# A second pair of feed-forward tiles by eight products, its token sums spread over it, and modulation tied to given VectorE operations

## The chip, the cores and the metric

The kernel runs on one core of a Trainium2 chip. The metric is the device time of one execution in microseconds (us), as the median of several runs; the profile and trace come from one further execution of the same program. Engine names are those of the profile: PE is TensorE, PEld its weight loads, DVE is VectorE, ACT is ScalarE, POOL is GpSimd, SP is SyncE, which issues the DMAs.

## The reference, cut to what matters

A trunk of two layers works on 512 latent and 256 context tokens, 1024 channels wide. Each layer is a feed-forward network (FFN), a token mixer and a second FFN. All have an RMS norm with a shift, scale and gate that come from a linear map of the conditioning vector (the "modulation"). The change touches the FFNs and the modulation alone:

```
def modulate(h, g, shift, scale):
    return rms_norm(h, g) * (1 + scale[:, None]) + shift[:, None]

def swiglu(h, w_in, w_out):
    a, b = jnp.split(h @ w_in, 2, axis=-1)
    return (jax.nn.silu(a) * b) @ w_out

mod_x = sc @ w_mod[l] + b_mod[l]                      # 9 groups of 1024 per layer
x = x + 0.5 * mx[2][:, None] * swiglu(modulate(x, norm_g, mx[0], mx[1]), ffn_in, ffn_out)
```

The inner width is 2816, which is 22 tiles of 128 rows. Four FFNs are computed; the last one (second FFN of the last layer) works on the 512 latent tokens alone, the other three on all 768.

## The kernel before, in words

**Number format.** Each operand is split into a high and a low part (`split`, L72: ACT copies the high part, DVE subtracts to get the low part), and each product is three matmuls (high by high, high by low, low by high). A weight of 128x512 that goes through `operand` (L167) so costs one ACT copy (`whi`) and one DVE subtraction (`wlo`). There are five rooms for such pairs, four for raw weights (L163), and six PSUM banks for products (L146).

**An FFN** (`ffn`, L449) goes over the 22 inner tiles in six parts of 2, 4, 4, 4, 4 and 4 (`PARTS`). For each part the input products make the gated tiles `g`, and then `out_product` (L296) multiplies them by eight output weights `j` and adds each result, times the gate `hg`, to the residual `X` (`resid`, L288, on DVE, which also frees the PSUM bank).

**Eight or seven products.** Part 0 goes by `ffn_tiles` (L320): plain products, in two stretches of tokens (512 and 256). Every later pair of tiles goes by `ffn_seven` (L381): the pair is a 2x2 block product (two tiles by two halves of the channels by two halves of the tokens), made of seven block products in place of eight. For that it needs sums of weights (POOL, rooms `ws`, L418 to L436) and sums of tokens. The token sums (`token_sums`, L345, once for each `k` of 0 to 3) are DVE operations on 128x384 (L356 and L359) with splits on ACT and DVE into the rooms `T`; one of them overwrites half of `h` itself in place (`hi[k][:, b]`, `lo[k][:, b]`). In program order the sums of `k` = 0, 1, 2 stand between `ffn_tiles` and the output products of part 0, those of `k` = 3 after its second output weight. The seven products stand in the order 1, 6, 5, 2, 7, 3, and product 4 is put off until after product 1 of the next one (`self.defer`).

**Modulation.** `mod_tile` (L193) loads 512 KB of `w_mod` through SP into one of two rooms `wm` and does two DVE operations (L200, `junk<-wm,cb`, 128x1024, with a sum of the row). The first FFN has 56 such tiles, of which the first eight (`early`) make its own gate `hg`, 40 go with the second FFN and 32 with the third, the last has none. They are told one after another by `background`, whose shares spread them over parts 1 to 5.

**The order of the work** on every engine is fixed when the program is built: the scheduler of the framework simulates the engines and puts on each, when it is free there, the first ready instruction in program order. What is ready early may so be placed far ahead of where it was told. On the chip each engine then runs its queue in that order.

The four FFNs are called A (layer 0, first), B (layer 0, second), C (layer 1, first) and D (layer 1, second) below; OUT0 is the output product of part 0, P1 to P5 are the parts 1 to 5, each with its input products and its output products. A mixer follows A and C; the weights of its first products are loaded and split on POOL (`start_mix`, L540) into space that `self.mod_room.close()` (L498) and the end of the rooms `T` give back.

Of the kernel before, what the change touches and what calls it, by code (L numbers as in the profile page):

```python
# [12 lines left out]
ALU = mybir.AluOpType  # L13
# [39 lines left out]
class Net:  # L53
# [182 lines left out]
    def norm_squares(self, sg):  # L236
# [3 lines left out]
        if self.hold:  # L240

            acc = self.mp.tile([128, 512], F32, tag="cb", name="acc", bufs=1)
        else:
            acc = self.wp.tile([128, 512], F32, tag="ws", name="acc", bufs=3)
# [73 lines left out]
    SPARE = ((("gp", "gh2", 1), ("gp", "gl2", 1)), (("gp", "gh3", 1), ("gp", "gl3", 1)), (("wp", "ws", 3), ("wp", "ws", 3)))  # L318

    def ffn_tiles(self, l, f, i0, g, h, segs):  # L320
# [13 lines left out]
        for sg in segs:  # L334
            for i in range(2):
                a, b = [self.product(ws[i, ab], h, sg, KD) for ab in range(2)]
                sa = self.ep.tile([128, 512], F32, tag="e", name="sa")[:, :sg.stop - sg.start]
                nc.scalar.activation(out=sa, in_=a, func=AF.Silu)
                nc.vector.tensor_tensor(sa, sa, b, op=ALU.mult)
                self.split(g[0][i][:, sg], g[1][i][:, sg], sa)  # L340
# [4 lines left out]
    def token_sums(self, h, nt, k):  # L345
# [8 lines left out]
        def whole(i, sl):  # L354
            z = self.ep.tile([128, NT // 2], F32, tag="c", name="t", bufs=8)[:, :m]
# [3 lines left out]
        sub = lambda o, x, y: nc.vector.tensor_tensor(o, x, y, op=ALU.subtract)  # L359
        t1, t3 = whole(k, a), whole(k, b)  # L360
# [3 lines left out]
        sub(t3, t2, t3)  # L364
        self.split(hi[k][:, b], lo[k][:, b], t3)
# [15 lines left out]
    def ffn_seven(self, l, f, i0, g, gi, B, nt, background):  # L381
# [4 lines left out]
        c = lambda n: self.ep.tile([128, NT // 2], F32, tag="c", name=n, bufs=8)[:, :m]  # L386
# [20 lines left out]
        for ab in range(2):  # L407
            r0, r1 = [self.raw(self.A["ffn_in"][l, f, i0 + i, ab], KD) for i in range(2)]
            a11, a12, a21, a22 = r0[:, 0:4], r0[:, 4:8], r1[:, 0:4], r1[:, 4:8]
            S = lambda: self.wp.tile([128, 4, 128], F32, tag="ws", name="ws", bufs=3)  # L410
# [11 lines left out]
            nc.vector.tensor_tensor(u2, s1, p6, op=ALU.add)  # L422
            mult(p5, self.operand(w1), 5, True, True)
# [3 lines left out]
            done(ab, "11", p1)  # L427
            w3 = S()
            nc.gpsimd.tensor_tensor(w3, a11, a21, op=ALU.subtract)
            mult(p6, self.operand(w3), 7, False, True)  # L430
# [4 lines left out]
            w4 = S()  # L435
            nc.gpsimd.tensor_tensor(w4, a12, w2, op=ALU.subtract)  # L436
            mult(p5, self.operand(w4), 3, False, True)
            nc.vector.tensor_tensor(u2, u2, p5, op=ALU.add)
            done(ab, "12", u2)
# [7 lines left out]
            background(1.0)  # L447
# [1454 lines left out]
```

## Time and profile before

| | us |
|---|---|
| median of 3 runs | 3454.74 (3453.64 to 3459.22) |
| profiled execution, its own time | 3451.14 |
| its span, first to last instruction | 3449.0 |

| engine | busy us | share of the span |
|---|---|---|
| PE | 3171.4 | 92% |
| DVE | 2502.3 | 73% |
| ACT | 1318.1 | 38% |
| POOL | 984.7 | 29% |

The profile counts an engine as busy while one of its instructions runs. A busy PE is not PE at its peak: its matmuls overlap, and their spacing tells the pace. The mean granted clock of TensorE is 0.936 of its full speed. The stages are told apart by the names of the tiles in the trace: input products read `hh`, `hl` or `T`, output products read `g`.

### The profile page before, as it was taken

The page shows a single profiled execution, that of the slowest core. Times are in us where ns is not written, and L with a number is a line of the kernel's source. Part 1 is how long each engine was busy: PE and PEld are TensorE (multiplying, and loading weights), DVE is VectorE, ACT ScalarE, POOL GpSimd, SP SyncE. Part 2 cuts the span into 40 slices and gives each one's busy share as a digit, 9 for nine tenths or more (in the row PEclk, how much of TensorE's full clock was granted, in tenths as well). Part 3 has the DMA queues.
Part 4 walks back from the last instruction along what each step waited for, and adds up shares of the span by engine and source line. Part 5 has one row for each costly group of instructions (what it writes and reads, how often), then busy time and mean ns, then how long its engine had stood idle before and what let it go on. Part 6 is the DMA issues. An engine that isn't in the chain of part 4 may idle for free.

```text
span 3449.0 us, 55188 instructions
## 1 busy us (share of the span) xinstructions
PE 3171.4 (92%) x20996; PEld 2810.6 (81%) x20996; DVE 2502.3 (73%) x4755; ACT 1318.1 (38%) x2399; POOL 984.7 (29%) x816
## 2 busy tenths in 40 slices
PE   7699999899989988899999799999899879989999
PEld 6688899778778766789998688999777667778998
DVE  8999856567955348998557899555747864468777
ACT  4332334442233334323335333333434233264444
POOL 0333334144332100433221133333245432103433
PEclk9899999899889888999999899999999878889999
DMA  6354322223232022343222243222313322033333
GB/s 244 119 168 153 114 68 77 95 77 99 71 112 64 5 90 94 123 158 126 71 74 80 97 148 123 70 68 66 121 55 107 88 79 55 5 109 100 99 98 123
DMA packets 184345, 335.77 MB, mean 97 GB/s; under 512 B 64752, under 2 KB 80976, under 8 KB 183696
## 3 DMA queue, kind: packets, MB, share of 16 engines
q1 hardware_dynamic: 184080, 332.25, 30.6%
q8 instruction: 165, 2.70, 0.3%
q14 instruction: 100, 0.82, 0.1%
HBM read 304.99 MB, written 27.18 MB: 96 GB/s over the span
## 4 chain that ended last, share of the span: by engine, by line
PE 61%; DVE 24%; issue 8%; DMA 4%; ACT 2%; POOL 1%; SPq 0%; DVEq 0%; ACTq 0%; POOLq 0%
PE pt L63 39%; PE pj L63 6%; PE pr L63 6%; DVE junk L200 5%; DVE wlo L78 4%; PE sc L63 3%; PE ps L63 1%; DVE T L1282 1%; DVE inv L1284 1%; PE po L63 1%; PE pc L63 1%; PE pg L63 1%; DVE gate L398 1%; DVE g L78 1%; DVE X L290 1%
## 5 line engine op out<-in xcount | busy, mean ns | idle before, releaser
L63 PE MATMUL pt<-g,whi 128*128 128x512 f32 (+1 forms) x2528 | 642.4, 345 | 49.1 <-DVE X L290 32.1
L77 ACT ACTIVATE whi<-wraw 128x512 fp32r<-128x512 f32 (+1 forms) x616 | 371.6, 615 | 571.2 <-PE pt L63 355.4
L63 PE MATMUL pt<-hh,whi 128*128 128x384 f32 (+2 forms) x1536 | 499.5, 336 | 58.9 <-DVE u L422 28.8
L63 PEld LDWEIGHTS pt<-g,whi 128*128 128x128 f32 x2528 | 441.3, 191 | 114.0 <-DVE X L290 33.8
L63 PE MATMUL pt<-hh,wlo 128*128 128x384 f32 (+2 forms) x1536 | 502.8, 331 | 14.3 <-DVE wlo L78 14.3
L63 PE MATMUL pt<-hl,whi 128*128 128x384 f32 (+2 forms) x1536 | 506.7, 332 | 2.5 <-DVE hl L78 2.5
L78 DVE TENSOR_TENSOR wlo<-wraw,whi 128x512 fp32r<-128x512 f32 (+1 forms) x528 | 424.4, 811 | 67.7 <-ACT whi L77 63.7
L63 PE MATMUL pt<-T,whi 128*128 128x384 f32 (+1 forms) x1920 | 455.1, 324 | 3.2 <-ACT whi L77 2.1
L63 PE MATMUL pt<-g,wlo 128*128 128x512 f32 (+1 forms) x1264 | 425.8, 342 | 0.0
L200 DVE SCALAR_TENSOR_TENSOR junk<-wm,cb 128x1024 bf16<-128x1024 f32 x272 | 363.5, 1336 | 11.3 <-ACT cb L191 10.4
L63 PEld LDWEIGHTS pt<-hh,whi 128*128 128x128 f32 x1536 | 299.2, 197 | 75.6 <-DVE u L422 34.4
L418 POOL TENSOR_TENSOR ws<-wraw 128x512 f32<-128x512 f32 x80 | 125.2, 1565 | 796.5 <-DMA wraw<-in_ffn_in 405.3
L63 PEld LDWEIGHTS pt<-T,whi 128*128 128x128 f32 x1920 | 334.9, 189 | 6.4 <-ACT whi L77 3.5
L290 DVE SCALAR_TENSOR_TENSOR X<-pt,hg,X 128x512 f32<-128x512 f32 (+1 forms) x376 | 226.9, 616 | 144.8 <-PE pt L63 144.0
L77 ACT ACTIVATE whi<-ws 128x512 fp32r<-128x512 f32 x320 | 200.0, 628 | 341.7 <-PE pt L63 257.4
L63 PEld LDWEIGHTS pt<-hh,wlo 128*128 128x128 f32 x1536 | 299.5, 196 | 21.5 <-DVE wlo L78 17.1
L63 PE MATMUL pt<-T,wlo 128*128 128x384 f32 (+1 forms) x960 | 307.9, 324 | 0.8 <-DVE wlo L78 0.7
L63 PEld LDWEIGHTS pt<-hl,whi 128*128 128x128 f32 x1536 | 301.3, 196 | 8.9 <-DVE hl L78 3.9
L78 DVE TENSOR_TENSOR wlo<-ws,whi 128x512 fp32r<-128x512 f32 x320 | 258.6, 811 | 52.2 <-ACT whi L77 48.5
L63 PEld LDWEIGHTS pt<-g,wlo 128*128 128x128 f32 x1264 | 241.3, 191 | 26.8
L433 POOL TENSOR_TENSOR s<-s,u 128x384 f32<-128x384 f32 (+1 forms) x80 | 107.3, 1341 | 471.3 <-DVE u L432 412.6
L78 POOL TENSOR_TENSOR wlo<-wraw,whi 128x512 fp32r<-128x512 f32 x88 | 126.1, 1435 | 300.6 <-ACT whi L77 262.9
(444 smaller groups left out, 5759.0 us busy)
## 6 DMA issues: line engine op xcount, KB each, us to landing
wraw<-in_ffn_in SPq DMA_DIRECT2D x176, 512.0 KB, 3.4
wm<-in_w_mod SPq DMA_DIRECT2D x144, 512.0 KB, 3.4
wraw<-in_ffn_out SPq DMA_DIRECT2D x192, 256.0 KB, 2.7
wraw<-in_w_in SPq DMA_DIRECT2D x88, 256.0 KB, 2.8
wraw<-in_w_out SPq DMA_DIRECT2D x32, 256.0 KB, 3.1
xd<-X SPq DMA_DIRECT2D x16, 384.0 KB, 2.5
wraw<-in_ffn_out SPq DMA_DIRECT2D x32, 128.0 KB, 2.2
wa<-in_w_out SPq DMA_DIRECT2D x16, 256.0 KB, 3.2
```

The lines of the kernel that those rows point to most:

```text
L63: self.nc.tensor.matmul(out, lhsT=lhsT, rhs=rhs, start=start, stop=stop, skip_group_check=skip)
L77: self.nc.scalar.activation(out=hi, in_=src, func=AF.Copy)
L78: (eng or self.nc.vector).tensor_tensor(lo, src, hi.bitcast(F32), op=ALU.subtract)
L200: nc.vector.scalar_tensor_tensor(out=junk, in0=w, scalar=1.0, in1=self.cb[:, s], op0=ALU.mult, op1=ALU.mult, accum_out=self.mod[l][:, s, j ...
L290: self.nc.vector.scalar_tensor_tensor(out=self.X[j][:, sg], in0=o, scalar=self.hg[l][:, s, 8 * n + j:8 * n + j + 1], in1=self.X[j][:, sg], ...
L398: nc.vector.tensor_tensor(gate[at], gate[at], src, op=ALU.mult)
L418: nc.gpsimd.tensor_tensor(w1, a21, a22, op=ALU.add)
L433: nc.gpsimd.tensor_tensor(s5, s5, u3, op=ALU.add)
L1282: nc.vector.tensor_tensor(tv, N[:, s, tt].unsqueeze(2).to_broadcast([96, nt, nj]), X[:, s, jj].unsqueeze(1).to_broadcast([96, nt, nj]), op ...
L1284: nc.vector.tensor_tensor(X[:, tt, jj], X[:, tt, jj], tv, op=ALU.add)
```

## The change

It does five things. (1) The first pair of part 1 (tiles 2 and 3) goes by a new `ffn_plain`, eight products without sums, in the two stretches of tokens. (2) The three token sums that go into `T` are told after the output weights j = 1, 3, 5, 7 of part 0, one `k` each; the one that overwrites `h` in place is told after `ffn_plain`, and takes two further additions for each `k`, since its inputs are made again. (3) `background` ties the DVE operations of what it tells behind the DVE instruction told last; it is called four times with a quarter share in each seven in place of once with a full share. (4) In a seven, product 3 comes ahead of product 7, and its weight sum ahead of that of 7. (5) Weight sums get four rooms in place of three, and DVE's small tiles `c` six in place of eight.

```diff
@@ token_sums(self, h, nt, k, ns)
+        if 3 in ns:
+            t2, t3 = whole(4 + k, b), whole(k, b)
+            sub(t3, t2, t3)
+            self.split(hi[k][:, b], lo[k][:, b], t3)
+            return
         t1, t3 = whole(k, a), whole(k, b)
         sub(t1, t3, t1)
         self.split(T[1][0][:, k, :m], T[1][1][:, k, :m], t1)
         t2 = whole(4 + k, b)
-        sub(t3, t2, t3)
-        self.split(hi[k][:, b], lo[k][:, b], t3)
         sub(t2, t2, t1)
...
@@ new
+    def ffn_plain(self, l, f, i0, g, gi, h, segs):
+        nc = self.nc
+        for i in range(2):
+            ws = []
+            for ab in range(2):
+                raw = self.raw(self.A["ffn_in"][l, f, i0 + i, ab], KD)
+                ws.append([self.operand(raw[:, 4 * q:4 * q + 4]) for q in range(2)])
+            for sg in segs:
+                self.gated(ws, h, sg, [g[q][gi + i][:, sg] for q in range(2)])
...
@@ ffn_seven
-            S = lambda: self.wp.tile([128, 4, 128], F32, tag="ws", name="ws", bufs=3)
+            S = lambda: self.wp.tile([128, 4, 128], F32, tag="ws", name="ws", bufs=4)
...
             nc.vector.tensor_tensor(u2, s1, p6, op=ALU.add)
+            background(0.25)
             mult(p5, self.operand(w1), 5, True, True)
...
             done(ab, "11", p1)
+            background(0.25)
+            w4 = S()
+            nc.gpsimd.tensor_tensor(w4, a12, w2, op=ALU.subtract)
             w3 = S()
             nc.gpsimd.tensor_tensor(w3, a11, a21, op=ALU.subtract)
+            mult(p5, self.operand(w4), 3, False, True)
+            nc.vector.tensor_tensor(u2, u2, p5, op=ALU.add)
+            done(ab, "12", u2)
+            background(0.25)
             mult(p6, self.operand(w3), 7, False, True)
...
-            background(1.0)
+            background(0.25)
@@ ffn
-        shares = [0.0, 2.0 * (len(PARTS) * 2 - 2) + 4.0 * (len(PARTS) - 2)]
+        shares = [0.0, 2.0 * (len(PARTS) * 2 - 3) + 4.0 * (len(PARTS) - 2)]
         def background(share):
             shares[0] += share
-            while side and todo - len(side) < todo * shares[0] / shares[1]:
-                side.pop(0)()
+            if side and todo - len(side) < todo * shares[0] / shares[1]:
+                told = self.nc.cur_bb.bb.instructions
+                last = next(x for x in reversed(told) if x.engine == mybir.EngineType.DVE)
+                with self.tc.issue_after(last):
+                    while side and todo - len(side) < todo * shares[0] / shares[1]:
+                        side.pop(0)()
...
-                for k in range(3):
-                    self.token_sums(h, nt, k)
-                sums = lambda j: self.token_sums(h, nt, 3) if j == 1 else None
+                sums = lambda j: self.token_sums(h, nt, j // 2, (1, 2, 4)) if j % 2 == 1 else None
             else:
                 for i in range(0, np_, 2):
-                    self.ffn_seven(l, f, m0 + i, g, i, B, nt, background)
+                    if m0 + i == 2:
+                        self.ffn_plain(l, f, m0, g, 0, h, segs)
+                        for k in range(4):
+                            self.token_sums(h, nt, k, (3,))
+                        B = self.token_blocks(h, nt)
+                    else:
+                        self.ffn_seven(l, f, m0 + i, g, i, B, nt, background)
```

Shared code of `ffn_tiles` and `ffn_plain` moves into `gated`: one product each for the two halves of the gate, SiLU on ACT, a DVE multiplication and a split.

## Rows read from the trace of the kernel before

**Rows 1.** The profile page, chain that ended last: shares of the span by line.
```profile
PE pt L63 39%; PE pj L63 6%; PE pr L63 6%; DVE junk L200 5%; DVE wlo L78 4%; PE sc L63 3%; PE ps L63 1%; DVE T L1282 1%; DVE inv L1284 1%; PE po L63 1%; PE pc L63 1%; PE pg L63 1%; DVE gate L398 1%; DVE g L78 1%; DVE X L290 1%
```

**Rows 2.** Stretches of A: OUT0, P1, P2, P3, P4.
```profile
core 0: us, PE busy (x) PEld busy (x) DVE busy (x) ACT busy (x) POOL busy (x), PEclk, DMA share, GB/s
79.40:126.60 47.20, 20.59 (x99) 16.73 (x98) 47.20 (x92) 12.09 (x26) 8.17 (x4) 0.75 0.35 114
126.60:226.20 99.60, 95.07 (x531) 89.25 (x530) 98.39 (x156) 31.92 (x60) 35.39 (x22) 0.98 0.49 153
226.20:328.60 102.40, 95.24 (x531) 88.92 (x530) 101.05 (x160) 31.90 (x60) 34.70 (x21) 0.98 0.47 153
328.60:430.10 101.50, 94.57 (x530) 89.21 (x529) 86.97 (x134) 31.79 (x60) 33.39 (x21) 0.98 0.38 124
430.10:522.00 91.90, 91.90 (x530) 87.92 (x529) 53.27 (x84) 32.85 (x60) 27.56 (x20) 1.00 0.22 69
```

**Rows 3.** The same view of B: OUT0, P1, P2.
```profile
1361.60:1390.00 28.40, 21.38 (x97) 16.56 (x96) 28.40 (x58) 8.73 (x21) 5.97 (x3) 0.88 0.39 132
1390.00:1500.90 110.90, 99.87 (x528) 92.41 (x529) 110.45 (x172) 35.29 (x66) 38.75 (x23) 0.94 0.41 134
1500.90:1602.20 101.30, 94.76 (x530) 89.17 (x529) 100.90 (x159) 32.03 (x60) 35.74 (x21) 0.98 0.49 154
```

**Rows 4.** The same view of C: OUT0, P1, P2.
```profile
1934.00:1964.50 30.50, 21.19 (x97) 16.22 (x95) 30.50 (x59) 9.92 (x23) 4.32 (x3) 0.90 0.36 117
1964.50:2076.00 111.50, 101.09 (x529) 93.66 (x530) 110.37 (x172) 33.92 (x64) 37.62 (x22) 0.92 0.42 136
2076.00:2175.70 99.70, 94.74 (x531) 89.09 (x530) 82.79 (x126) 32.27 (x60) 31.95 (x20) 0.98 0.37 118
```

**Rows 5.** The same view of D: OUT0, P1, P2.
```profile
3106.10:3120.70 14.60, 13.13 (x51) 10.46 (x52) 14.60 (x38) 5.53 (x14) 0.00 (x0) 0.88 0.31 100
3120.70:3189.90 69.20, 64.32 (x431) 59.52 (x430) 55.03 (x81) 30.51 (x63) 31.63 (x24) 0.98 0.32 102
3189.90:3253.30 63.40, 62.02 (x433) 58.03 (x432) 48.77 (x77) 29.25 (x60) 26.78 (x20) 1.00 0.32 100
```

**Rows 6.** Input products of P3 and P4, output products of P4 (FFN A).
```profile
328.60:392.50 63.90, 56.97 (x315) 55.58 (x314) 63.90 (x95) 23.80 (x46) 25.65 (x15) 0.97 0.39 123
430.10:484.40 54.30, 54.30 (x315) 54.30 (x314) 32.72 (x50) 25.14 (x47) 19.28 (x14) 1.00 0.18 55
484.40:522.00 37.60, 37.60 (x217) 33.62 (x216) 20.55 (x34) 7.71 (x13) 8.28 (x6) 1.00 0.29 91
```

**Rows 7.** P3 of A, modulation (tile junk) alone: us, DVE busy (records), clock, DMA.
```profile
328.60:430.10 101.50, 30.40 (x44) 0.98 0.38 124
```

**Rows 8.** DVE in order of time, OUT0 of A: start, us, instruction.
```profile
101.73 3.15 DVE L359 TENSOR_TENSOR t<-t 128x384 f32<-128x384 f32 x2
...
111.54 0.16 DVE L216 TENSOR_SCALAR hg<-mod 128x16 f32<-128x16 f32 x1
...
112.76 2.18 DVE L290 SCALAR_TENSOR_TENSOR X<-pt,hg,X 128x512 f32<-128x512 f32 x4
```

**Rows 9.** Groups of DVE instructions, 1340 to 1390 us (B, end of norm and OUT0).
```profile
L200 DVE SCALAR_TENSOR_TENSOR junk<-wm,cb 128x1024 bf16<-128x1024 f32 x12 | 15.1, 1262 | 5.7 <-ACT cb L191 5.7
L359 DVE TENSOR_TENSOR t<-t 128x384 f32<-128x384 f32 x12 | 7.4, 620 | 0.0
```

**Rows 10.** The profile page, the modulation's DVE group over the whole span.
```profile
L200 DVE SCALAR_TENSOR_TENSOR junk<-wm,cb 128x1024 bf16<-128x1024 f32 x272 | 363.5, 1336 | 11.3 <-ACT cb L191 10.4
```

**Rows 11.** Waits of SP's queue, 126 to 400 us: total us, times, longest.
```profile
SPq L60 <- DVE junk L200: 133.3, 45, 6.5
```

**Rows 12.** SP, POOL and PE in order of time: first weights of A's mixer, first product.
```profile
391.42 0.80 SPq L60 DMA_DIRECT2D gS<-in_w_in  x2
...
595.15 1.65 POOL L78 TENSOR_TENSOR wh<-wa,wh 128x512 fp32r<-128x512 f32 x1
...
619.96 0.71 PE L63 MATMUL pj<-hh,wh 128*128 128x512 f32 x2 [2.94 <-ACT hh L77]
```

More of the change, by code (lines that the diff above doesn't have):

```diff
@@ L243, in norm_squares @@
         else:
-            acc = self.wp.tile([128, 512], F32, tag="ws", name="acc", bufs=3)
+            acc = self.wp.tile([128, 512], F32, tag="ws", name="acc", bufs=4)
         nc.scalar.activation(out=acc[:, :n], in_=self.X[0][:, sg], func=AF.Square)
@@ L315, in out_and_norm, with gated @@
         return h
-    SPARE = ((("gp", "gh2", 1), ("gp", "gl2", 1)), (("gp", "gh3", 1), ("gp", "gl3", 1)), (("wp", "ws", 3), ("wp", "ws", 3)))
+    SPARE = ((("gp", "gh2", 1), ("gp", "gl2", 1)), (("gp", "gh3", 1), ("gp", "gl3", 1)), (("wp", "ws", 4), ("wp", "ws", 4)))
+    def ffn_plain(self, l, f, i0, g, gi, h, segs):
[7 more added lines that the diff above has]
+                self.gated(ws, h, sg, [g[q][gi + i][:, sg] for q in range(2)])
+    def gated(self, ws, h, sg, out):
+        nc = self.nc
+        a, b = [self.product(w, h, sg, KD) for w in ws]
+        sa = self.ep.tile([128, 512], F32, tag="e", name="sa")[:, :sg.stop - sg.start]
+        nc.scalar.activation(out=sa, in_=a, func=AF.Silu)
+        nc.vector.tensor_tensor(sa, sa, b, op=ALU.mult)
+        self.split(*out, sa)
     def ffn_tiles(self, l, f, i0, g, h, segs):
@@ L335, in ffn_tiles, with token_sums @@
             for i in range(2):
[L336 to L340, printed above, removed]
+                self.gated([ws[i, ab] for ab in range(2)], h, sg, [g[q][i][:, sg] for q in range(2)])
     def token_rooms(self):
         self.T = {n: [self.tp.tile([128, 4, NT // 2], F32R, tag=f"T{n}{q}", name="T") for q in range(2)] for n in (1, 2, 4)}
-    def token_sums(self, h, nt, k):
+    def token_sums(self, h, nt, k, ns):
         nc = self.nc
@@ L354, in whole @@
         def whole(i, sl):
-            z = self.ep.tile([128, NT // 2], F32, tag="c", name="t", bufs=8)[:, :m]
+            z = self.ep.tile([128, NT // 2], F32, tag="c", name="t", bufs=6)[:, :m]
             nc.vector.tensor_tensor(z, hi[i][:, sl].bitcast(F32), lo[i][:, sl].bitcast(F32), op=ALU.add)
@@ L385, in ffn_seven @@
         a, b = slice(0, m), slice(m, nt)
-        c = lambda n: self.ep.tile([128, NT // 2], F32, tag="c", name=n, bufs=8)[:, :m]
+        c = lambda n: self.ep.tile([128, NT // 2], F32, tag="c", name=n, bufs=6)[:, :m]
         bank = lambda: self.pj.tile([128, 512], F32, tag="pj", name="pt")[:, :m]
@@ L434, in ffn_seven @@
             done(ab, "22", s5)
[L435 to L439, printed above, removed]
             def last(ab=ab, p6=p6, s1=s1, op=self.operand(a22)):
@@ L490, in ffn @@
                 self.out_product(l, n, src, g, np_, segs if nt == NT else [slice(0, nt)], between=sums)
-            if part == 0:
-                B = self.token_blocks(h, nt)
             m0 += np_
```

## The prediction

> **What bounds the kernel now.** I read the chain of waits first. PE's products lead it, but modulation on DVE (line 200) holds 5% of the span and the low parts of weights (line 78) another 4% [rows 1]. So there are places where PE waits for DVE, and the next view must say where. The table of stretches does. A part that nothing disturbs is P4 of A: 91.9 us, PE busy throughout, clock 1.00, DVE busy for 53.3 [rows 2]. P1, P2 and P3 of A hold the same matmuls (about 530) and take 99.6, 102.4 and 101.5, with DVE busy for 98.4, 101.1 and 87.0 [rows 2]. P3 shows why: its 22 modulation operations take 30.4 us [rows 7] and all lie in its input products, which have 32.7 us of other DVE work (that of P4's). 32.7 + 30.4 = 63.1, and the stretch takes 63.9 with DVE busy for all of it, against 54.3 in P4 [rows 6]. The stretch is as long as its DVE work. P4 has no modulation at all: it is bunched in the first parts because the schedule places it as soon as it is ready.
>
> The worst place is OUT0. Its bare time: P4's output stretch of 37.6 us holds 192 output matmuls and 24 of 384 columns; 384 columns cost 54.3 / 312 = 0.174 (315 records, three cut by the edges), so the 192 cost 37.6 - 4.2 = 33.4 [rows 6], and OUT0, with half as many, 16.7. In D, with the 512-column two thirds alone, it is 11.1.
>
> Excess over bare, all DVE-bound (DVE busy 100% of OUT0 in all four) [rows 2 to 5]:
> OUT0: A 47.2 - 16.7 = 30.5; B 11.7; C 13.8; D 3.5; together 59.5.
> P1 to P3: A 7.7 + 10.5 + 9.6 = 27.8; B 19.0 + 9.4 = 28.4; C 19.6 + 7.8 = 27.4 (bare 91.9 each); D 69.2 - 63.4 = 5.8; together 89.4.
> In all 148.9 us that PE loses to DVE. The mixers are not touched.
>
> **What the change adds: PE work.** The plain pair is 4 weight tiles by 8 blocks by 3 matmuls, 96 of 512 and 96 of 256 columns. These are the shapes and the number of a whole output stretch: 33.4 us. The seven that it replaces is 2 x 7 x 12 = 168 of 384 columns: 29.2. That is +4.2 in A, B and C, and two thirds of it, 2.8, in D: **+15.4 us**, on the path in full, since PE sets it there.
>
> **Token sums.** Before, twelve DVE operations for each k, at about 0.62 us [rows 9], must end before the first seven: 48 in all, some 30 us per FFN in front of and inside OUT0. Now ten for each k stay there; two (the sum that overwrites h, and its low part) go behind the plain pair, with two additions made anew. So about 5 us leave OUT0 and 4 x 4 x 0.62 = 10 us come back behind the plain pair, where product 7, five products later (10 us), is the first to read them. The plain pair itself gives 33 us of PE time with little DVE work: 8 low parts of weights and 8 gate operations, against 14 and more in a seven. That hides what is left of the sums. Were the cover gone, the 10 us would fall on PE; I take 0. POOL loses one pair's weight sums, and these no longer run beside the token sums. In OUT0 of A two token operations took 3.15 us together [rows 8], where POOL had 8.2 us of work [rows 2], against 0.62 each [rows 9].
>
> OUT0 of A is special: residual additions need the gate hg, which is ready at 111.5, and the first four follow at 112.8 [rows 8]. DVE is full until then with the eight early modulation tiles and the sums. Only the 5 us of sums, some collisions and the later modulation between the residual additions go: I take 10.5 of 30.5 (bounds 5 and 20). B: 12 modulation operations, 15.1 us [rows 9], and 5 us of sums leave the end of the norm and OUT0; I take 8 of OUT0's 11.7 and 3 in the norm before it, 11. C by analogy: 9 and 3, 12. D has no modulation and gains by the sums and the plain pair alone: 3.5 + 5.8 to 3.0, a gain of 6.3. **Together 39.8.**
>
> **Modulation tied and spread.** One operation costs 30.4 / 22 = 1.38 us with its accumulator read [rows 7]. The shares give 8/34 of the tiles to each of P2, P3, P4, half of it to the input products. For A (48 tiles) that is 11.3 tiles, 31.2 us of DVE: inputs 32.7 + 15.6 = 48.3 of 54.3 us, outputs 20.6 + 15.6 = 36.2 of 37.6. B (40 tiles): 45.7 and 33.6. C (32): 43.1 and 31.0. By these sums DVE fits under PE everywhere, in A's output stretches by little, where six PSUM banks let PE run ahead. An in-order queue will not be perfect; I leave 2 us in each of four parts of A, 7 in B and 6 in C: 27.8 + 28.4 + 27.4 - 21 = **62.6 gained** (bounds: all 83.6, and half of it).
> The waits that this adds: a modulation operation must follow the DVE instruction told before it; behind it queue the next low part of a weight and the next u, s or residual addition, and behind those PE. Its load moves with it on SP: room wm is free only after the tile two before, and raw weights queue behind that wait. SP already waits so, 45 times, at most 6.5 us [rows 11]; the raw weights have four rooms, two seven-steps' worth, so nothing.
>
> A rule speaks against the spreading. Two-input DVE operations and POOL: the row shows modulation at 1.34 us on average [rows 10] and 1.26 in a stretch with little POOL work [rows 9]. The Trainium skill, page "SBUF — State Buffer", section "Who interferes with whom", says that a DVE instruction with two SBUF inputs and a GpSimd instruction that reads SBUF exclude each other, the second blocked until the first ends. By that, 11 operations moved beside POOL's sums in P4 or P5 cost a whole POOL operation each at worst; by the rows the mean cost is 0.1 each and lies in my 1.38 already.
>
> **Small ones.** Product 3 ahead of 7 leaves product 4 only one product (2.1 us) after the DVE read of 7's bank, where it had two: cost 0 to 0.3 a seven, taken as 0, as P4 shows DVE idle for 40%. A fourth room of weight sums: POOL is at 19.3 of 54.3 [rows 6], no bound: 0. Six small DVE tiles for eight: a seven holds six at most: 0 (at worst 1 us a seven). The first weights of A's mixer were loaded at 391 [rows 12], when modulation had ended; now its room frees only with P5's inputs, near the end of A's inputs. POOL ended at 597 and PE needed it at 620 [rows 12], 23 us of cover for some 5 to 10: 0, else 10 each in A and C.
>
> **The sum.** 39.8 + 62.6 - 15.4 = 87.0. The profiled execution took 3451.1, so 3364.1. It stands 3.6 below the median of the runs, so **3368** for the median.
>
> **Rivals.**
> (a) *The queue keeps OUT0 as it is.* Token sums are ready as soon as the norm is, and the schedule already places them before they are told; it may go on putting them ahead of the residual additions. Then OUT0 gives nothing and P1 to P3 half: 89.4 / 2 - 15.4 = 29, **3425**. For it: DVE ran sums before the first residual addition in A [rows 8]. Against it: residual additions and the first sums change places in program order, and modulation leaves the stretch.
> (b) *All of it goes:* 148.9 + 6 for the norms - 15.4 = 139.5, **3315**. Against it: A's gate is late whatever is done with the sums.
> (c) *Slower.* Tied operations stand right in front of urgent ones. The place is the input products of P2 to P5; the price is x for each of the 240 tied operations (2 x 120 tiles), on PE, in place of the 83.6 lost now. Break-even: 240 x = 83.6 + 39.8 - 15.4 = 108, x = 0.45 us, a third of an operation. P3 of A pays 9.6 / 22 = 0.44 each today, so that is not far off if spreading brought nothing. At x = 0.7: 168 - 83.6 - 39.8 + 15.4 = +60, **3515**. Against it: at 48.3 of 54.3 there is slack for each, which P3 had not.
> (d) *The tie does nothing* (the operations are still bunched): the parts keep their loss but for the sums in P1, some 20 back, with 39.8: 44 net, 3410. I count it with (a).
>
> **How the numbers follow.** Forecast 0.60, own range 3340 to 3405 (A's OUT0 from 5 to 20, the spreading's residue from 10 to 40). (a) with (d) 0.18, (b) 0.12, (c) 0.10. The range of 8 in 10 reaches from half of (b) to past (a): **3325 to 3435**. A measurement of this kernel tells about 0.2% (7 us) from no change. Faster: 0.60 + 0.18 + 0.12 less a little of (a), 0.88; the same 0.03; slower 0.09.
>
> **What would show it.** Right: OUT0 of B and C near 20 us with residual additions from its first microseconds; P2 to P4 of A, B and C alike, 92 to 95 us, with DVE at 75 to 90%; modulation to the end of P5; P1 about 98. OUT0 of A still near 36, until hg. Wrong: parts of 97 us and more through P4 and P5 with PE waiting for low parts or for u and s behind modulation, which is (c); OUT0 unchanged with sums in front, which is (a); or a late first product of the mixer.

## Result: 97.2% of the time before, and where it came from

The changed kernel takes **3358.6 us** (median; 3354.4 to 3362.7), the kernel before, timed beside it, 3456.0. The ratio is **0.9717, interval 0.970 to 0.9735**. The forecast was 3368 in a range of 3325 to 3435. The profiled execution took 3361.9, span 3360.0, against 3449.0.

The chain of waits (the profile's walk back from the last instruction, at each step to what held it up) comes first again, from the profile page of the changed kernel:

```profile
PE 71%; DVE 16%; DMA 5%; ACT 3%; issue 3%; POOL 1%; SPq 1%; DVEq 0%; POOLq 0%; ACTq 0%
PE pt L63 49%; PE pj L63 7%; PE pr L63 6%; PE sc L63 3%; DVE wlo L78 2%; PE ps L63 2%; DVE junk L200 2%; PE po L63 1%; DVE T L1310 1%; DMA wraw<-in_ffn_in 1%; DVE inv L1312 1%; PE pc L63 1%; DVE X L290 1%; PE pg L63 1%; ACT t L278 1%
```

PE has 71% of the chain in engines. Modulation has gone from 5% to 2% of it and the low parts of weights from 4% to 2% [rows 1]. The stretches of A after, in the columns of [rows 2]: OUT0, P1, P2, P3, P4.

```profile
79.80:123.50 43.70, 23.26 (x98) 18.86 (x97) 41.54 (x85) 10.00 (x22) 0.00 (x0) 0.73 0.34 111
123.50:219.50 96.00, 96.00 (x554) 88.19 (x553) 67.08 (x105) 29.20 (x54) 23.94 (x16) 1.00 0.32 99
219.50:315.40 95.90, 93.71 (x530) 89.41 (x530) 87.44 (x136) 32.70 (x60) 34.59 (x20) 0.98 0.41 132
315.40:409.50 94.10, 92.18 (x531) 87.91 (x530) 83.89 (x132) 32.96 (x60) 32.98 (x20) 1.00 0.40 130
409.50:502.90 93.40, 92.14 (x530) 87.84 (x529) 85.67 (x133) 32.89 (x60) 30.66 (x20) 1.00 0.41 131
```

P2 to P4 are alike now, 93 to 96 us with DVE busy for 84 to 87, where they took 102.4, 101.5 and 91.9 with 101.1, 87.0 and 53.3. P1 is PE from end to end. OUT0 has hardly moved. The same view of B (OUT0, P1, P2) and of D (P2 alone), for [rows 3] and [rows 5]:

```profile
1344.00:1365.40 21.40, 18.01 (x99) 14.80 (x97) 21.40 (x47) 8.16 (x19) 0.00 (x0) 1.00 0.34 106
1365.40:1461.50 96.10, 96.10 (x553) 88.30 (x554) 76.05 (x122) 29.25 (x55) 26.13 (x16) 1.00 0.32 104
1461.50:1554.60 93.10, 91.96 (x530) 87.62 (x529) 78.16 (x123) 32.87 (x60) 30.05 (x20) 1.00 0.39 125
...
3088.90:3154.00 65.10, 62.46 (x434) 58.18 (x433) 49.93 (x77) 29.44 (x61) 27.01 (x21) 1.00 0.31 98
```

B's OUT0 fell to 21.4 and its P1 from 110.9 to 96.1. D's P2 did not fall: 65.1, where it took 63.4.

The table divides the profiled executions. An FFN runs here from the first matmul of its OUT0 to the last of P5. "Mixer A" and "mixer C" are what lies between A and B and between C and D, with the norms and the input products of the next part 0; the 53.2 and 49.2 us between B and C are a norm and such input products.

| us | before | after | difference |
|---|---|---|---|
| A: OUT0, P1 to P3, P4 and P5 | 47.0, 303.5, 184.5 | 43.5, 286.0, 186.0 | -19.5 |
| B, the same | 29.9, 305.1, 184.3 | 20.8, 281.5, 185.7 | -31.3 |
| C, the same | 32.7, 303.3, 184.3 | 21.5, 280.1, 186.8 | -31.9 |
| D: OUT0, P1, P2 to P5 | 14.4, 69.3, 255.5 | 13.0, 65.4, 267.6 | +6.8 |
| norm between B and C | 53.2 | 49.2 | -4.0 |
| mixer A, mixer C | 744.4, 654.4 | 748.6, 640.7 | +4.2, -13.7 |

The FFNs give 75.9 us, less than the forecast's 87 for FFNs and norms. The mixers, which the change does not touch, give 9.5 of the rest and the norm 4.0. So the forecast was close for reasons that are partly not its own, and three questions were put to the chip: which part of the change brings the gain, what D lost, and why the mixers moved.

### The profile page after: what moved, and what is told of

Its sections match the earlier page's. It is cut to its first block, busy times and chain, and to the rows that moved or that the text cites. A ratio compares the mean times of both kernels' runs of the same rounds, so it can differ in the third digit from the quotient of the medians.

```text
span 3360.0 us, 55161 instructions
## 1 busy us (share of the span) xinstructions
PE 3140.3 (93%) x21092; PEld 2787.7 (83%) x21092; DVE 2465.8 (73%) x4731; ACT 1304.0 (39%) x2359; POOL 932.3 (28%) x776
## 4 chain that ended last, share of the span: by engine, by line
PE 71%; DVE 16%; DMA 5%; ACT 3%; issue 3%; POOL 1%; SPq 1%; DVEq 0%; POOLq 0%; ACTq 0%
PE pt L63 49%; PE pj L63 7%; PE pr L63 6%; PE sc L63 3%; DVE wlo L78 2%; PE ps L63 2%; DVE junk L200 2%; PE po L63 1%; DVE T L1310 1%; DMA wraw<-in_ffn_in 1%; DVE inv L1312 1%; PE pc L63 1%; DVE X L290 1%; PE pg L63 1%; ACT t L278 1%
## 5 line engine op out<-in xcount | busy, mean ns | idle before, releaser
L63 PE MATMUL pt<-hh,whi 128*128 128x384 f32 (+2 forms) x1664 | 531.9, 329 | 36.3 <-ACT g L77 19.0
L63 PE MATMUL pt<-hl,whi 128*128 128x384 f32 (+2 forms) x1664 | 541.9, 327 | 0.7 <-DVE hl L78 0.6
L63 PE MATMUL pt<-hh,wlo 128*128 128x384 f32 (+2 forms) x1664 | 536.9, 326 | 0.5 <-DVE wlo L78 0.3
L63 PE MATMUL pt<-T,whi 128*128 128x384 f32 (+1 forms) x1728 | 406.0, 322 | 0.0
L436 POOL TENSOR_TENSOR ws<-wraw 128x512 f32<-128x512 f32 x72 | 113.3, 1574 | 1036.4 <-DMA wraw<-in_ffn_in 915.1
L63 PEld LDWEIGHTS pt<-hh,whi 128*128 128x128 f32 x1664 | 318.7, 193 | 51.7 <-ACT g L77 21.1
L63 PEld LDWEIGHTS pt<-hl,whi 128*128 128x128 f32 x1664 | 321.0, 193 | 10.8 <-DVE hl L78 1.8
L63 PEld LDWEIGHTS pt<-hh,wlo 128*128 128x128 f32 x1664 | 319.1, 193 | 9.4 <-DVE wlo L78 1.3
L63 PEld LDWEIGHTS pt<-T,whi 128*128 128x128 f32 x1728 | 300.0, 188 | 1.0
L63 PE MATMUL pt<-T,wlo 128*128 128x384 f32 (+1 forms) x864 | 276.4, 322 | 0.0
L63 PE MATMUL pj<-hh,whi 128*128 128x512 f32 x616 | 191.2, 376 | 15.0 <-DVE k L1126 8.3
```

The lines of the kernel that those rows point to most:

```text
L63: self.nc.tensor.matmul(out, lhsT=lhsT, rhs=rhs, start=start, stop=stop, skip_group_check=skip)
L436: nc.gpsimd.tensor_tensor(w1, a21, a22, op=ALU.add)
```

## Experiments

Times are medians of the timed runs, ratios stand to the kernel before. Stage figures are from one profiled execution each, divided as above; how far a stage that no edit touches can differ between two traces is told under "Why the mixers move".

**Which part gives the gain: the tie.** The tie of modulation behind a DVE instruction is taken out of the changed kernel, all else stays:

```diff
-                told = self.nc.cur_bb.bb.instructions
-                last = next(x for x in reversed(told) if x.engine == mybir.EngineType.DVE)
-                with self.tc.issue_after(last):
-                    while side and todo - len(side) < todo * shares[0] / shares[1]:
-                        side.pop(0)()
+                while side and todo - len(side) < todo * shares[0] / shares[1]:
+                    side.pop(0)()
```

> The changed kernel without the tie: modulation is told at the same places, but the schedule may place it as early as it is ready. Theory: it is bunched again in the first parts; P2 and P3 of A and P2 of B and C go back to 99 to 102 us (some 36 more together), and OUT0 and P1 of B and C lose 5 to 10 each to modulation in front: 3400 to 3420. Rival (the plain pair alone makes the gain, the tie does nothing): 3359 within 8.

Measured: 3434.6, ratio 0.9927 (0.990 to 0.995). More is lost than expected. The stretches P1 to P4 of A without the tie:

```profile
125.20:227.60 102.40, 97.69 (x554) 87.99 (x553) 98.78 (x158) 27.86 (x54) 27.39 (x16) 1.00 0.51 161
227.60:330.20 102.60, 95.46 (x530) 89.30 (x529) 102.35 (x163) 31.57 (x60) 35.42 (x21) 0.98 0.48 154
330.20:430.60 100.40, 94.55 (x531) 89.35 (x530) 77.58 (x119) 32.41 (x60) 33.36 (x20) 0.98 0.33 108
430.60:522.50 91.90, 91.90 (x531) 87.93 (x530) 53.94 (x84) 33.23 (x60) 27.32 (x20) 1.00 0.21 69
```

This is the picture of [rows 2]: DVE nearly full in P1 and P2, and P4 with no modulation at all. Quarter shares alone do not spread it. The other way round, the tie with the quarter shares put into the kernel before, without the plain pair, the spread sums, the new order and the new rooms:

```diff
-            while side and todo - len(side) < todo * shares[0] / shares[1]:
-                side.pop(0)()
+            if side and todo - len(side) < todo * shares[0] / shares[1]:
+                told = self.nc.cur_bb.bb.instructions
+                last = next(x for x in reversed(told) if x.engine == mybir.EngineType.DVE)
+                with self.tc.issue_after(last):
+                    while side and todo - len(side) < todo * shares[0] / shares[1]:
+                        side.pop(0)()
...
-            background(1.0)
+            background(0.25)
```

> The kernel before with the tie and the quarter shares alone: no plain pair, sums, order and rooms as before. Theory: P2 and P3 of A and P2 of B and C come to 93 to 95 us (33 less together), OUT0 and P1 of B and C give back the 12 to 20 modulation operations that stood there, some 15 to 20 each, A's P1 5; D stays: 3456 - 70 = 3385, range 3370 to 3405. Rival (modulation costs the same wherever it stands): 3456 within 10.

Measured: 3350.2, ratio 0.9692 (0.966 to 0.972), better than expected and no worse than the whole change. OUT0, P1 and P2 of A:

```profile
80.20:124.60 44.40, 19.95 (x97) 16.26 (x97) 42.79 (x82) 12.01 (x26) 7.07 (x5) 0.77 0.30 98
124.60:216.70 92.10, 92.10 (x531) 87.86 (x530) 84.25 (x128) 32.59 (x60) 33.63 (x21) 1.00 0.40 126
216.70:308.70 92.00, 92.00 (x530) 87.81 (x529) 85.38 (x131) 32.51 (x60) 34.99 (x20) 1.00 0.41 132
```

The parts are at their bare 92 us with DVE busy for 84 to 85: a tied operation costs PE nothing here. Of the FFNs, the tie with its quarter shares takes off 82.9 us (A 29.7, B 23.4, C 29.1, D 0.7), the rest without the tie 12.3, both together 75.9. They overlap, and beside the tie the other four parts cost 7 us. The fourth room, told below, costs more than that: with three rooms the four FFNs take 1819.1 us, against 1830.8 with the tie alone.

**The plain pair.** The first pair goes by seven again; tie, spread sums and rooms stay:

```diff
                     if m0 + i == 2:
-                        self.ffn_plain(l, f, m0, g, 0, h, segs)
                         for k in range(4):
                             self.token_sums(h, nt, k, (3,))
                         B = self.token_blocks(h, nt)
-                    else:
-                        self.ffn_seven(l, f, m0 + i, g, i, B, nt, background)
+                    self.ffn_seven(l, f, m0 + i, g, i, B, nt, background)
```

> The changed kernel with the first pair of part 1 by seven products, token sums still spread over OUT0, the one in place told behind OUT0. Theory: PE has 15.4 us less work, but the sums are due at the end of OUT0 again: 10 us of sums and what is left of the others stand in front of the first seven, 6 to 10 us a FFN, so 24 to 40 for four: 3367 to 3385, slower than the changed kernel. Rival (with modulation gone the sums fit into OUT0, and the plain pair is paid for nothing): 3343 within 4.

Measured: 3373.6, ratio 0.9752 (0.973 to 0.978), as the theory said. P1 of B:

```profile
1343.80:1449.00 105.20, 97.32 (x531) 91.74 (x530) 95.96 (x147) 36.84 (x68) 37.33 (x25) 0.95 0.32 102
```

With the pair it takes 96.1, PE busy throughout. In C it is 102.5 against 96.5, in D 76.5 against 65.4. In A, where the sums are done before P1 begins, P1 is 91.9 without the pair and 96.0 with it: in that stretch it only adds its own work, 4.1 us. Over the whole FFN the pair gains 15.1 us in B, 3.5 in C and 12.3 in D, and costs A 7.9 (515.6 against 507.7). In A, OUT0 is 47.4 without the pair and 43.5 with it, but P2, P3 and P4 are 91.9 each without it and 95.9, 94.1 and 93.4 with it. The pair takes no tied modulation, so P1 holds 23.1 us of it in place of 31.2 and the later parts hold more; that this is what makes them longer was not tested. The medians differ by 15.0 us where the four FFNs differ by 23.1, as mixer A took 734.0 in that trace.

**The place of the token sums.** They are told ahead of the output products again, plain pair and all else as changed:

```diff
-                sums = lambda j: self.token_sums(h, nt, j // 2, (1, 2, 4)) if j % 2 == 1 else None
+                for k in range(3):
+                    self.token_sums(h, nt, k, (1, 2, 4))
+                sums = lambda j: self.token_sums(h, nt, 3, (1, 2, 4)) if j == 1 else None
```

> The changed kernel with one part undone: the token sums of k = 0, 1, 2 told ahead of the first output weight of part 0 again and those of k = 3 after the second, in place of one k after each second weight. Plain pair, tie, order and rooms stay. My theory: the tie is what emptied OUT0, the place of the sums counts little (with the tie alone and the sums in front OUT0 of B was 24.8 and of C 21.7): OUT0 of B and C 21 to 25, A 43 to 45, P1 as it is (96 to 97), a median of 3358 to 3366. Rival: the sums in front hold back the first residual addition as before the change; OUT0 of B and C back at 28 to 32, the median at 3372 to 3382.

Measured: 3360.8, ratio 0.9719 (0.970 to 0.974). OUT0 is 43.8, 21.5, 21.5 and 13.0 us in A to D, where the change has 43.5, 20.8, 21.5 and 13.0. With the tie and the plain pair, where the sums are told counts for nothing.

**A's gate.** Why is OUT0 of A still 43.5? DVE in order of time after, and PE's wait there and in the kernel before:

```profile
102.62 1.21 DVE L200 SCALAR_TENSOR_TENSOR junk<-wm,cb 128x1024 bf16<-128x1024 f32 x1
...
108.07 0.15 DVE L216 TENSOR_SCALAR hg<-mod 128x16 f32<-128x16 f32 x1
...
109.55 3.22 DVE L290 SCALAR_TENSOR_TENSOR X<-pt,hg,X 128x512 f32<-128x512 f32 x6
```

```profile
PEld pt L63 <- DVE X L290: 16.6, 1, 16.6
```

```profile
PEld pt L63 <- DVE X L290: 22.8, 1, 22.8
```

The gate comes at 108.1 (111.5 before [rows 8]), since its early modulation tiles still stand among token sums, which the schedule drew ahead: OUT0 of A holds 41 operations of token sums, 22.1 us, where it held 36, 22.7 us. What left it is modulation, 13 operations before and 6 after. Even of the sums told behind the plain pair only the four low parts (`hl`), which overwrite `h`, stand in P1. One wait of PE for the first residual additions is 16.6 us long (the row gives total, times, longest); the last fence shows 22.8 before the change. Here the token sums of A are tied behind the DVE operation that makes `hg`, so that they can't be drawn ahead of it:

```diff
+                gate = next(x for x in reversed(self.nc.cur_bb.bb.instructions) if x.engine == mybir.EngineType.DVE)
+
+                def sums(j):
+                    if j % 2 == 1:
+                        with self.tc.issue_after(gate) if early else ExitStack():
+                            self.token_sums(h, nt, j // 2, (1, 2, 4))
```

> The changed kernel with the token sums of FFN A tied behind the DVE operation that makes its gate hg; all else as changed. Theory: in A the gate alone sets OUT0 (PE waits 16.4 us once, for the first residual addition), and it is late because sums stand between the early modulation operations; with the sums behind it OUT0 of A falls from 43.5 to about 30, and the sums go under the plain pair: P1 stays at 96 to 99, the time 3349, range 3343 to 3354. Rival: DVE has the same work in all, so P1 grows by what OUT0 loses: 3359 within 4.

Measured: 3344.5, ratio 0.9678 (0.965 to 0.970). OUT0 and P1 of A, and the gate:

```profile
82.10:104.90 22.80, 18.59 (x97) 16.04 (x96) 21.58 (x47) 6.22 (x13) 0.00 (x0) 0.93 0.44 150
104.90:201.00 96.10, 96.10 (x554) 88.23 (x553) 90.05 (x146) 32.46 (x61) 28.78 (x16) 1.00 0.33 105
```

```profile
89.58 0.17 DVE L216 TENSOR_SCALAR hg<-mod 128x16 f32<-128x16 f32 x1
```

OUT0 gives 20.7 us, more than was expected, and P1 takes none back, since the plain pair covers the sums. The median fell by 14 alone; in the profiled execution mixer C is 12.5 longer, 653.2 (see below). The same tie without the plain pair, on the kernel with the tie of modulation alone:

```diff
+                gate = next(x for x in reversed(self.nc.cur_bb.bb.instructions) if x.engine == mybir.EngineType.DVE)
...
-                for k in range(3):
+                for k in range(0 if early else 3):
                     self.token_sums(h, nt, k)
```

> The tie alone (kernel before, tied modulation) with A's token sums told over OUT0 and tied behind its gate; no plain pair, so the sums are due right after OUT0. Theory: OUT0 of A falls from 44.4 by some 12, but 40 to 48 sum operations (25 to 30 us) then stand between the gate and the first seven with 10 us of output products over them, so P1 grows by 10 to 15: no gain, 3350 within 5. Rival: the sums fit under OUT0's rest: 3340.

Measured: 3359.8, ratio 0.9710 (0.968 to 0.974). OUT0 falls by 21.0 to 23.4, and P1 rises by 17.5 to 109.6. A as a whole is 3.5 us shorter than with the tie alone (501.9 against 505.4). The median is 10 longer, outside what was expected; in the traces the difference lies in mixer A, 752.5 against 739.3. So the plain pair is worth 13.5 us in P1 of A once the sums come after the gate (96.1 against 109.6), and costs 4 there while they come before it. Over the whole of A that is a gain of 7.4 (494.5 against 501.9) and a cost of 7.9.

**The order of products 3 and 7.** D was slower after, and my first suspect was product 4, which has one product less between itself and the read of its bank:

```diff
-            mult(p5, self.operand(w4), 3, False, True)
...
             mult(p6, self.operand(w3), 7, False, True)
...
+            mult(p5, self.operand(w4), 3, False, True)
```

> The changed kernel with product 7 ahead of product 3 again, as before the change; the rest as changed. Theory: the new order costs FFN D its parts P2 to P5, since after product 7 the chain half-sum on POOL, gate on DVE, high part on ACT has one product less before the next weight's high part queues behind it on ACT; input stretches of 40.4 to 42.7 us go back to 38.8, 11 to 12 us for D, and A, B, C stay within 1 us each: about 3347. Rival: the six small tiles, or the later release of the raw weights, cost D its time; then the order gives nothing and the time stays at 3359 within 4.

Measured: 3347.1, ratio 0.9678 (0.965 to 0.971). The number came out and the theory fell: D is 348.6, as slow as with the change. The 13 us came from mixer A (735.8 in place of 748.6), which has neither product; what that is worth is told under "Why the mixers move".

**The rooms.** Next, three rooms for weight sums, six small tiles kept; then three rooms and eight small tiles, as before the change:

```diff
-            S = lambda: self.wp.tile([128, 4, 128], F32, tag="ws", name="ws", bufs=4)
+            S = lambda: self.wp.tile([128, 4, 128], F32, tag="ws", name="ws", bufs=3)
```

> The changed kernel with three rooms of weight sums as before, six small tiles as changed. FFN D grew by 7 us with the change and stayed so when the order of products 3 and 7 was undone; left are the rooms. Theory: the six small tiles cost D its time (a seven holds four, and the gate of the one before up to four more), so D stays at 345 to 349, A, B and C within 2 us: 3359 within 6. Rival: the fourth room makes the schedule place weight sums ahead of half-sums on POOL; then D goes back to 337 to 339 and the time to 3350.

> The changed kernel with three rooms of weight sums and eight small tiles, both as before (four rooms and eight tiles do not fit together). Theory: D goes back to 336 to 340 (parts of 63.4), some 8 us, the time to 3351 within 5. Rival (neither room is the cause, D's time is the order of products together with the sums): D stays at 345 or more.

Measured: 3338.1, ratio 0.9654 (0.963 to 0.968), with three rooms; 3362.8, ratio 0.9731 (0.971 to 0.976), with eight tiles as well. D falls from 345.9 to 331.2 and 333.8: the theory of the small tiles fell, and **the fourth room costs D 14.7 us**. Eight tiles make OUT0 longer (B 25.4, C 24.3, D 16.2), and both mixers came out long in that run (754.0 and 650.0), which is why its median misses the 3351 that was expected.

Why would one more room cost time? POOL in order of time, in a part of D, after; the last brackets are idle time before the instruction and what ended it:

```profile
3169.24 1.29 POOL L451 TENSOR_TENSOR ws<-wraw 128x512 f32<-128x512 f32 x1 [0.63 <-DVE wlo L78]
3174.84 1.29 POOL L436 TENSOR_TENSOR ws<-wraw 128x512 f32<-128x512 f32 x1 [4.32 <-DMA wraw<-in_ffn_in]
3176.09 0.73 POOL L459 TENSOR_TENSOR s<-s,u 128x256 f32<-128x256 f32 x1
```

and what follows on DVE and on PE's weight loads:

```profile
3176.86 1.50 DVE L416 TENSOR_TENSOR gate<-gate,s 128x256 f32<-128x256 f32 x1 [2.19 <-POOL s L459]
```

```profile
3183.03 0.19 PEld L63 LDWEIGHTS pt<-hh,whi 128*128 128x128 f32 x1 [2.77 <-ACT g L77]
```

With three rooms, POOL at the same place of a part of D:

```profile
3163.24 1.34 POOL L451 TENSOR_TENSOR ws<-wraw 128x512 f32<-128x512 f32 x1 [2.23 <-DVE wlo L78]
3164.55 1.18 POOL L459 TENSOR_TENSOR s<-s,u 128x256 f32<-128x256 f32 x1
3165.69 1.48 POOL L436 TENSOR_TENSOR ws<-wraw 128x512 f32<-128x512 f32 x1
```

L436 is the first weight sum of the next step, L451 the last one of this step, L459 this step's addition to `s5`. With three rooms L451 waits for a room until DVE has split an earlier sum (2.23 us idle), and L459 follows it before L436. With four rooms L451 runs earlier, POOL is free earlier, and the order built has L436 ahead of L459. In the trace L436 then waits 4.32 us for its raw weights. L459 stands behind it until 3176.09, though its last input is there at 3173.28 (DVE, `u` of L458: 0.41 us from 3172.87). DVE waits for L459, its queue is late from there on, and PE waits some 6 us later for `g`. That reading says what should mend D with four rooms kept: the addition must leave POOL's queue.

```diff
-            nc.gpsimd.tensor_tensor(s5, s5, u3, op=ALU.add)
+            nc.vector.tensor_tensor(s5, s5, u3, op=ALU.add)
```

> The changed kernel, four rooms kept, with the one addition of a seven that POOL does (s5 and u3, 128x384 or 128x256, 0.73 us in D) put on DVE. In the parts P2 to P5 of D the trace after shows POOL's queue as: first weight sum of the next pair (4.32 us of waiting for its raw weights), then this addition, then DVE 2.19 us idle for it, then PE 2.8 us idle for g. With three rooms the addition stands ahead of that sum. My theory: the fourth room costs D its 14.7 us by this order alone; without the addition on POOL, P2 to P4 of D fall from 65 to 67 us to 63 to 64, D from 346 to 332 to 336 (DVE has room for 0.4 us each), A, B and C stay within 4 us each: a median of 3344 to 3352. Rival: it is the fourth room's other effect that costs D (the raw weights held longer, the sums made earlier beside DVE's work): D stays at 343 to 350, the median at 3355 to 3365.

Measured: 3343.9, ratio 0.9672 (0.965 to 0.970). D is 334.5, P3 and P4 62.7 and 62.8, A to C within 4 us. PE's waits for `g` in D, P1 to P5, after, with three rooms, and with the addition on DVE:

```profile
PEld pt L63 <- ACT g L77: 11.1, 4, 2.8
```

```profile
PEld pt L63 <- ACT g L77: 3.7, 4, 0.9
```

```profile
PEld pt L63 <- ACT g L77: 5.0, 4, 2.1
```

The theory holds for most of it: with the addition off POOL, 11.4 of the 14.7 us are gone. What is left is nearly all in P2, 65.5 against 62.8 with three rooms, and was not looked into. The wait rows differ by 7.4 us between four rooms and three; another 5.1 us, three times 1.7, is PE at a lower clock around three of the four waits (last section).

**Together.** Three rooms and the sums behind A's gate; then the same with product 7 ahead of 3:

> The changed kernel with three rooms for weight sums (as in the run with three rooms) and the token sums of A tied behind its gate (as in the run with the sums behind the gate). My theory: the two edits act in different places and add. FFN stages: A 494.5 and B 488.3 to 488.7, C 487.3 to 488.4 from the two runs, D 331.2; together 1801 against 1819 with three rooms alone. All else as with three rooms (80 + 747.9 + 49.4 + 639.2 + 3.7 = 1520), so a span of 3321 and a median of 3320. Rival: both kernels with that tie so far had a mixer that was 13 us longer (C 653.2 in the one, A 752.5 in the other); then 3333 and no gain worth the name over the 3338 of three rooms alone.

> As the run with three rooms and the gate, with product 7 ahead of product 3 again. My theory: the order of the two products is worth nothing in the FFNs (within 4 us over all four stages), and a mixer's time is drawn anew with each build, so this comes within 15 us of that run on either side, by its mixers alone. Rival: the mixer of A was 735.8 in the one run with that order and the new parts, 12.8 shorter than with the order of the change; if that hangs on the order, it comes back here and the median is 12 lower, at some 3308.

Measured: 3332.7, ratio 0.9639 (0.962 to 0.966), and **3322.8, ratio 0.9611 (0.959 to 0.963)**, the best of all. The two edits add: the four FFNs take 1799.0 us, 1801 were expected, and 1819.1 with three rooms alone. But mixer C is long again, 654.3 (mixer A 739.2), so the median is that of the rival. The order of the products is worth nothing in the FFNs (1798.9), and mixer A is short with either order (737.5 here), so it does not hang on that.

**Why the mixers move.** No edit touches them. In these runs mixer A took 734 to 754 us and mixer C 639 to 654. The same instructions are there, but the schedule is drawn anew with each build, and for mixer C the time goes with the order. In five builds (the change, products 7 and 3 as before, three rooms, sums bunched, addition on DVE) its instructions stand in the same order on every engine, and it took 639.2 to 643.1 us. In the three with both the plain pair and the sums behind the gate they stand in another order, the same in all three, and it took 650.5 to 654.3. The stretches of mixer C, after and with the sums behind the gate (first 440 us, a middle part, the last 120.6):

```profile
2369.70:2809.70 440.00, 383.72 (x3023) 309.44 (x3022) 287.71 (x691) 170.33 (x276) 159.02 (x150) 0.88 0.29 86
2809.70:2889.70 80.00, 78.98 (x875) 62.26 (x873) 28.69 (x74) 33.26 (x58) 17.72 (x32) 0.94 0.06 12
2889.70:3010.30 120.60, 105.36 (x681) 86.02 (x678) 78.27 (x212) 57.51 (x121) 3.21 (x8) 0.87 0.25 78
```

```profile
2348.00:2788.00 440.00, 383.43 (x2994) 307.45 (x2992) 284.15 (x684) 169.40 (x274) 160.20 (x150) 0.88 0.29 86
2788.00:2880.50 92.50, 91.42 (x912) 71.88 (x912) 32.25 (x80) 35.11 (x61) 17.72 (x32) 0.83 0.06 10
2880.50:3001.20 120.70, 104.70 (x669) 84.83 (x667) 78.98 (x212) 56.99 (x120) 3.20 (x8) 0.90 0.24 78
```

The outer parts are cut equally long, and do not hold quite the same matmuls (the x columns). Cut so, the 12.5 us lie in the middle part, where PE is busy nearly all the time in both; its granted clock there is 0.83 in place of 0.94. Over all three stretches the time lost to the clock, (1 - clock) x us, is 73.3 and 80.6, so the clock makes about 7 of the 12.5. In all runs together mixer C took 639 to 643 us at a mean clock of 0.89, and 650 to 654 at 0.87 or 0.88. Which change of order lowers the clock was not tried.

Mixer A moves without any such change. In four builds (the change, products 7 and 3 as before, sums behind the gate, three rooms with that gate) its instructions stand in the same order on every engine, and it took 748.6, 735.8, 746.8 and 739.2 us. The same stretch of mixer A with products 7 and 3 as before and with the sums behind the gate:

```profile
1206.30:1258.90 52.60, 45.74 (x202) 31.69 (x202) 19.07 (x41) 24.66 (x47) 0.00 (x0) 0.97 0.36 126
```

```profile
1195.90:1255.80 59.90, 52.79 (x203) 36.41 (x203) 19.43 (x40) 25.30 (x47) 0.00 (x0) 0.83 0.32 115
```

The same matmuls take 52.6 us at a clock of 0.97 and 59.9 at 0.83: 7.3 of the 11.0 us between these two mixers lie here. Single executions of one kernel differ as much: with the sums behind the gate the four took 3342.3 to 3352.3, and the trace is of the longest. So the 13 us of mixer A that the run on the order of products seemed to gain do not come from an order of instructions in it, and one trace each can't tell them from what differs between two executions of one kernel. The medians of these two kernels do lie 11.5 us apart, so something of the build may last; why the clock was granted otherwise stays open.

## Why the forecast was right, step by step

**What bounds it: right.** P1 to P3 were as long as their DVE work, and spreading the modulation took that away.

**The tie and the spread: right, and the residue too large.** 62.6 were forecast with 21 left in the parts. P1 to P5 of A to C fell by 58.9 us, and the plain pair's 12.6 lie in them: 71.5 gained. The residue is 12, not 21: B and C have parts at 91.8. With the tie alone A's parts have next to none (91.9 to 92.1), and what they have after the change came with the plain pair. DVE's sums for the parts held too: 45.7 + 33.6 = 79.3 us for a part of B were forecast, P2 shows 78.2.

**OUT0 of A: wrong, and below its lower bound.** 10.5 was forecast (5 to 20), 3.5 came. The step that failed is that some 5 us of sums would leave OUT0 because they are told later: 22.1 us of sums stand in it, where there were 22.7. Of what is told behind the plain pair, the additions and differences were ready and were drawn ahead; only the four low parts stand in P1. Rival (a) described it, for all four FFNs; it held in A alone, where the gate needs DVE while the sums are ready. The run with the sums behind the gate shows 20.7 to be had.

**OUT0 of B and C: right in size, for another reason.** 8 and 9 were forecast, 9.1 and 11.2 came, 4 of the norm's 3. But the sums' new place has no part in it, as told above. Modulation leaving the stretch is what was priced at 15.1 us [rows 9], and it left by the tie.

**The plain pair: right in P1, and not priced behind it.** 4.2 us on the path: P1 of A is 96.0, PE busy for all of it, against a bare 91.9. Its cover for the late sums, left out of the sum as free, held: PE is busy for all of P1 in A and in B. That P2 to P4 of A would be 7.7 us longer together with the pair than without it was not forecast, nor that OUT0 would be 3.9 shorter.

**Small ones: one of four wrong.** The fourth room was taken as 0, since POOL was "no bound" by its busy time. It cost 14.7 us in D, 11.4 of them through an addition that stands behind a waiting sum in POOL's queue. That is why D's P2 to P5 grew by 12.1 us, while its OUT0 and P1 gave 5.3 where 3.5 was forecast. A's and C's first mixer products begin 5.4 and 5.5 us after the FFN's last, as before (5.4 and 5.5): the 0 there holds. So does the 0 for the order of the products. Six tiles cost nothing; in the one run with eight, OUT0 was longer.

**POOL beside DVE.** The modulation operations, spread beside POOL's sums, take 1.360 us on average:

```profile
L200 DVE SCALAR_TENSOR_TENSOR junk<-wm,cb 128x1024 bf16<-128x1024 f32 x272 | 370.0, 1360 | 0.5
```

That is 0.024 more than in [rows 10]; the rows decided, and the rule's worst case did not come. Yet single rows show such a block: the `gate` row above takes 1.50 us, from 3176.86 to 3178.36, where the same operation takes 0.41 at 3182.17, and POOL's second weight sum (L437, 1.29 us) ran from 3176.79 to 3178.08. This agrees with the Trainium skill, page "SBUF — State Buffer", section "Who interferes with whom": a DVE instruction with two SBUF inputs and a GpSimd instruction that reads SBUF exclude each other.

**The mixers: "not touched", and yet moved.** They and the norm between B and C gave 13.5 us, the norm's 4.0 forecast as 3, the mixers' 9.5 not forecast at all. Without the mixers' 9.5 the execution would have taken 3371; with D as forecast too (a net gain of 3.5 in place of a loss of 6.8) 3361, against a sum of 3364.1 and a measured 3361.9. The miss in D (10.3) and the mixers' gift (9.5) cancel, and so, nearly, do the 7.0 us by which OUT0 of A fell short and the 8.9 that the spreading gave beyond its forecast. That the sum came within 3 us is luck; that it came near 87 of gain is the tie.

**Rivals.** (a) fell but for A, (b) too: 3315 is below all, though three further edits reach 3323. (c) fell: a tied operation costs nothing in A with the tie alone. (d) is refuted by the two runs on the tie.

## To carry to other kernels

When an engine's list of work is fixed at build time, telling an instruction later does not make it later: what is ready is drawn ahead. A tie to an instruction of the same engine does, and here that one edit, with its quarter shares, was worth the whole gain. A further buffer is no gift: ask which instruction it lets into an in-order queue, what that waits for, and what stands behind it. And read each stage of the two traces, not the total: parts of 10 us that nobody edited, and that differ even with the same order of instructions, can make a wrong theory look right.

## What was not expected of the hardware

A short wait of PE can cost clock as well, and the clock can fall without one. PE's granted clock around the 2.77 us wait in D after:

```profile
3180.00:3183.00 3.00, 0.46 (x4) 0.26 (x3) 3.00 (x6) 0.38 (x2) 1.71 (x2) 1.00 0.30 85
3183.00:3185.00 2.00, 1.94 (x15) 1.97 (x16) 2.00 (x3) 1.92 (x6) 0.72 (x1) 0.89 0.00 0
3185.00:3187.00 2.00, 2.00 (x11) 2.00 (x11) 1.74 (x4) 0.33 (x1) 0.72 (x1) 0.50 0.50 131
3187.00:3189.00 2.00, 2.00 (x15) 2.00 (x14) 1.11 (x2) 1.35 (x3) 0.33 (x1) 0.75 0.00 0
3189.00:3192.00 3.00, 3.00 (x28) 3.00 (x27) 1.86 (x4) 2.02 (x5) 0.00 (x0) 1.00 0.27 87
```

After the wait PE runs at full clock first, then at 0.50, the lower of its two levels (1.2 and 2.4 GHz), while busy all the time, and is back at 1.00 by 3189. By these rows the clock takes 0.2 + 1.0 + 0.5 = 1.7 us more for a wait of 2.8. D after has four such waits. Two others go with a fall to half clock as well (0.50 from 3249.5 to 3252.5, and 0.61 from 3316.9 to 3320.4), but the first, as long as they are, is not:

```profile
3115.20:3117.80 2.60, 0.03 (x1) 0.02 (x1) 2.60 (x6) 0.43 (x2) 1.31 (x2) 1.00 0.21 81
3117.80:3120.00 2.20, 2.19 (x18) 2.20 (x19) 2.20 (x4) 2.12 (x5) 0.68 (x1) 1.00 0.06 15
3120.00:3123.00 3.00, 3.00 (x27) 3.00 (x26) 2.65 (x5) 1.85 (x5) 1.06 (x1) 1.00 0.26 87
```

So such a wait is not enough by itself. Nor is it needed. In the mixer, with the sums behind the gate, 8 us of PE busy throughout at full clock come first, and the clock falls late in the next microsecond (0.90 is the mean of it), in which PE is idle for 0.11 us:

```profile
2822.00:2830.00 8.00, 8.00 (x99) 6.70 (x98) 3.18 (x8) 2.52 (x5) 4.28 (x6) 1.00 0.12 20
2830.00:2831.00 1.00, 0.89 (x17) 0.64 (x13) 1.00 (x4) 0.51 (x1) 0.94 (x1) 0.90 0.00 0
2831.00:2838.00 7.00, 6.18 (x86) 5.93 (x87) 2.81 (x7) 0.98 (x3) 0.01 (x1) 0.50 0.07 12
```

What decides is not shown by these runs.
